# Where the left operands of a seven-product projection are summed and split

## The chip, the cores and the metric

The kernel runs on one core of a Trainium2 chip. The metric is device time in microseconds (us), the median over several runs of the same kernel. The engines are called as in the profile: PE is TensorE (PEld its weight loads), DVE VectorE, ACT ScalarE, POOL GpSimd, SP SyncE, which here only issues DMAs.

## The reference, cut to what matters

One layer of a hybrid decoder trunk is computed in float32: token mixers (gated linear attention, a short convolution, dilated attention), their merge, and then a feed-forward part. The change concerns the feed-forward alone, with 1024 tokens, width 1024 and 2816 hidden channels:

```python
h = rmsnorm(x, pre_ffn_g[l])
gt = causal_dwconv(h @ w_ff_gate[l], ff_conv_w[l]) + ff_conv_b[l]
y = (jax.nn.gelu(gt, approximate=True) * (h @ w_ff_up[l])) @ w_ff_down[l]
x = x + rmsnorm(y, post_ffn_g[l])
```

## The kernel before, in words

**Split.** TensorE gets each float32 operand as two parts, h and l, and a product takes three matmuls: h with h, h with l, l with h. `split` makes the parts: an ACT copy into h (L157), then a DVE subtraction into l (L158).

**Seven of eight.** Large products are taken in 2 x 2 blocks by Winograd's form, with seven block products in place of eight. For that the operands are summed first (A21 + A22, and so on). A block product in the first stage has twelve matmuls of 128 x 128 by 128 x 512.

**First stage: the hidden channels.** The 2816 hidden channels are eleven pairs of 128-channel tiles. Pair 0 is done by plain products (`gemm_by_part`, `gate_or_value`) while `block_sums` makes the sums T1..T4 of the tokens' blocks (tiles FT). Then, for pairs c = 1 to 10, `seven` runs twice: on w_ff_gate (the gate unit) and on w_ff_up (the up unit). One call of `seven`

- loads two 0.5 MB pieces of weights into `raw` tiles (SP issues them; there are three such tiles),
- makes seven left operands: POOL sums blocks of them (L278, L280, L282, L284; into `fb` or in place), and `split` puts them into one of two sets of wh and wl,
- runs seven products into the PSUM banks X, Y and Z. Five reads of a bank stand between products that use the same bank: ACT copies X, Z and X into places of `ring` (L301, L306, L309), DVE adds Y, Z and X to these (L303, L312, L314). So the fifth product of a unit, which writes Z again, cannot start before ACT's read L306 is done; the last cannot before DVE's L314,
- leaves its seventh product for later: it runs right after the first product of the next unit.

As the four blocks (0,0), (0,1), (1,1), (1,0) of a gate unit come out, `conv` makes the convolution and gelu (ACT L1273, DVE L1274 to L1278, ACT L1279). In an up unit DVE multiplies the gate's result by each block (L1314), and the two tiles y of a pair are written to DRAM, to `d_act` (L1317), 0.5 MB each.

**Last stage: back to the model's width.** `down` takes groups of pairs, (0,1), (2,3,4), (5,6,7), (8,9,10), and for each group seven block products in the order 1, 2, 5, 6, 3, 7, 4. For each pair it loads the activations from d_act and the rows of w_ff_down (L1380, all on SP's queue), sums both operands on POOL in place (L1392), splits both (L157, L158) into one of twelve places `ops` (four of them are the tiles wh and wl), and runs the matmuls (L1433): four tiles of tokens, three matmuls for each tile and pair. The result of each tile is added to `acc` by DVE (L1439; in the first group partly copied by ACT, L1438). With the last group `finish` makes the closing norm and residual sum for each of the eight tiles of tokens.

**What sets the order.** The language's scheduler puts the instructions of each engine into one order; each engine then takes its queue in that order and waits on semaphores. `issue_after` in `down` keeps the splits ahead from standing before the sums of results already done (LEAD = 3 products).

## Time and profile before

| what | value |
|---|---|
| time, median of 3 runs (range) | 2009.29 us (2007.48 to 2010.98) |
| span of the profiled execution | 2004.0 us |
| share of the span busy: PE / DVE / ACT / POOL | 95% / 67% / 44% / 38% |
| DMA traffic over the span | 110 GB/s |
| first stage, pairs 1 to 10 | from about 1371 to 1751.56 us of the span |
| last stage, with the finish | from 1751.56 to 2004.0 us |

The profile is of one execution. The device time of that execution is not given apart from its span; the median of the runs is 5.3 us above the span, so what lies around the span is taken as these 5.3 us. Times such as 1536.68 are microseconds from the start of the span. A row of a timeline is one instruction (or x of them run together): its start, its duration, engine, line, operation, out<-in, and in brackets how long the engine was idle before it and what ended that. The rows of PE in a timeline overlap, since matmuls are pipelined: the distance between two starts is what one costs. The shares of busy time are averages over stages with different limits; the stages are read apart below.

### The profile page before, as it was taken

The numbers are of one execution on the slowest core, as the hardware profiler recorded it, in microseconds if no ns is written. First come the engines' busy times: TensorE is split into PE (matmuls) and PEld (weight loads), VectorE is DVE, ScalarE is ACT, GpSimd is POOL, SyncE is SP. The second block draws the span as 40 slices with busy tenths as digits, with TensorE's granted clock in tenths as the row PEclk, the third lists the DMA queues.
The fourth block names the chain that finished last, engine by engine and source line by source line (L and its number), as shares of the span: only waits on it lengthen the run. The fifth ranks groups of instructions, "written<-read, shape, count | busy, mean of one in ns | idle before, by whom it ended". The sixth has DMA issues, their size and how long they took to land. (4 is left out here: it accounts for less than half of the span.)

```text
span 2004.0 us, 25969 instructions
## 1 busy us (share of the span) xinstructions
PE 1902.5 (95%) x9705; PEld 1602.2 (80%) x9705; DVE 1342.6 (67%) x1998; ACT 879.6 (44%) x1620; POOL 764.4 (38%) x456
## 2 busy tenths in 40 slices
PE   6999999999989999999999998998999999989995
PEld 5988788877777899899688776887888888877874
DVE  8756744378888433577545487577666666689998
ACT  5433444455444322435356623344444444454443
POOL 4532323265655331102214562024332322257674
PEclk9999999999999999999999998999999999999998
DMA  4121323323222524213467554221222221443114
GB/s 172 63 84 65 120 95 116 114 97 108 103 84 99 157 77 149 64 38 101 135 202 227 145 190 137 91 88 64 74 95 76 82 95 64 156 160 126 51 76 147
DMA packets 160141, 219.77 MB, mean 110 GB/s; under 512 B 27025, under 2 KB 118031, under 8 KB 160016
## 3 DMA queue, kind: packets, MB, share of 16 engines
q1 hardware_dynamic: 160016, 218.12, 32.8%
q8 instruction: 76, 1.25, 0.3%
q14 instruction: 49, 0.40, 0.1%
HBM read 160.27 MB, written 57.82 MB: 109 GB/s over the span
## 5 line engine op out<-in xcount | busy, mean ns | idle before, releaser
L158 DVE TENSOR_TENSOR wl<-raw,wh 128x512 fp32r<-128x512 f32 (+1 forms) x214 | 211.1, 1019 | 144.9 <-ACT wh L157 144.8
L294 PE MATMUL sX<-T,wh 128*128 128x512 f32 x720 | 227.4, 397 | 17.0 <-DVE ring L314 16.3
L157 ACT ACTIVATE wh<-raw 128x512 fp32r<-128x512 f32 (+1 forms) x226 | 146.3, 671 | 90.2 <-PE sX L294 67.8
L294 PEld LDWEIGHTS sX<-T,wh 128*128 128x128 f32 x720 | 136.1, 191 | 51.6 <-DVE ring L314 22.6
L294 PE MATMUL sX<-FT,wh 128*128 128x512 f32 x480 | 148.1, 390 | 0.9 <-DVE ring L314 0.9
L294 PE MATMUL sX<-T,wl 128*128 128x512 f32 x360 | 141.8, 394 | 0.0
L505 POOL TENSOR_TENSOR fr<-fr 128x512 f32<-128x512 f32 x48 | 72.4, 1507 | 96.3 <-ACT fr L498 92.1
L278 POOL TENSOR_TENSOR fr<-raw 128x512 f32<-128x512 f32 x30 | 40.2, 1339 | 179.9 <-issue 69.1
L278 POOL TENSOR_TENSOR fb<-raw 128x512 f32<-128x512 f32 x20 | 25.8, 1290 | 216.3 <-DMA raw<-in_w_ff_gate_dram 69.2
L158 DVE TENSOR_TENSOR wl<-fr,wh 128x512 fp32r<-128x512 f32 x90 | 64.8, 742 | 63.0 <-ACT wh L157 62.3
L294 PEld LDWEIGHTS sX<-FT,wh 128*128 128x128 f32 x480 | 89.9, 188 | 20.2 <-DVE ring L314 1.6
L157 ACT ACTIVATE wh<-fr 128x512 fp32r<-128x512 f32 (+1 forms) x97 | 62.2, 658 | 81.2 <-PE sX L294 48.1
L294 PE MATMUL sX<-FT,wl 128*128 128x512 f32 x240 | 93.4, 389 | 0.0
L1433 PE MATMUL fX<-ops 128*128 128x512 f32 x336 | 85.4, 399 | 8.2 <-DVE acc L1439 8.2
L1433 PEld LDWEIGHTS fX<-ops 128*128 128x128 f32 x336 | 64.2, 192 | 23.4 <-DVE acc L1439 6.4
L284 POOL TENSOR_TENSOR raw<-raw 128x512 f32<-128x512 f32 x50 | 80.4, 1609 | 0.0
L294 PEld LDWEIGHTS sX<-T,wl 128*128 128x128 f32 x360 | 68.7, 191 | 14.7
L506 DVE TENSOR_TENSOR ring<-ring,fr 128x512 f32<-128x512 f32 x48 | 58.4, 1216 | 28.4 <-POOL fr L505 26.8
L294 PE MATMUL sZ<-T,wh 128*128 128x512 f32 x240 | 73.9, 389 | 0.0
L158 DVE TENSOR_TENSOR ops<-src,ops 128x512 fp32r<-128x512 f32 x77 | 71.7, 967 | 0.0
L1433 PE MATMUL fZ<-ops 128*128 128x512 f32 x264 | 67.5, 398 | 3.8 <-DVE ops L158 2.1
L301 ACT ACTIVATE ring<-sX 128x512 f32<-128x512 f32 x48 | 28.5, 594 | 96.1 <-PE sX L294 75.0
(548 smaller groups left out, 5695.9 us busy)
## 6 DMA issues: line engine op xcount, KB each, us to landing
raw<-in_w_in_dram SPq DMA_DIRECT2D x48, 512.0 KB
raw<-in_w_gate_dram SPq DMA_DIRECT2D x24, 512.0 KB
d_sig<-ring SPq DMA_DIRECT2D x48, 256.0 KB
d_qk<-ring SPq DMA_DIRECT2D x48, 256.0 KB
raw<-in_w_ff_gate_dram SPq DMA_DIRECT2D x22, 512.0 KB
raw<-in_w_ff_up_dram SPq DMA_DIRECT2D x22, 512.0 KB
src<-d_act SPq DMA_DIRECT2D x22, 512.0 KB
src<-in_w_ff_down_dram SPq DMA_DIRECT2D x22, 512.0 KB
```

The source lines that it names most:

```text
L157: S.activation(h, src, AF.Copy)
L158: eng.tensor_tensor(l, src, h.bitcast(F32), op=OP.subtract)
L278: G.tensor_tensor(s1, A21, A22, op=OP.add)
L284: G.tensor_tensor(A21, A11, A21, op=OP.subtract)
L294: PE.matmul(ps, a[x][:, k], b[y][:, k], start=first and k == 0 and n == 0, stop=k == 3 and n == 2, skip_group_check=not first)
L301: S.activation(c11, X, AF.Copy)
L505: G.tensor_tensor(sw, sw, sin[:, hs], op=OP.mult)
L506: V.tensor_tensor(as_(o), as_(o), perm(sw), op=OP.add)
L1433: PE.matmul(ps, o[:, a, ts], o[:, b], start=start and j == 0 and x == 0, stop=j == n - 1 and x == 2, skip_group_check=not start)
```

## The change

The left operands of the last stage's products (of the activations) are no longer made there. They are made in the first stage, as a pair's blocks come out of the up unit: `forms` sums them on POOL in place in the tiles y, `keep` splits each of the seven (ACT copy, DVE subtraction) into one of four staging places and writes h and l together to a new DRAM array `d_fa`, 0.5 MB for each product. The staging places are the rows k = 0 to 3 of F[1] (names F1h, F1l), which nothing reads once `block_sums` is done. `forms` is called as follows: after block (0,0), product 1; after block (1,1), products 4, 5, 7, 6 with the sums a21+a22, a11-a21, s-a11; after block (1,0), product 2, the sum for 3, product 3. For pair 0 all of it runs after `block_sums`. The array d_act and its two writes for each pair are gone.

In the last stage `down` loads h and l of a left operand from d_fa right into the place `ops`, one 0.5 MB load for each pair and product, and sums and splits the right operand alone. The weights' tiles `src` are now six places of one pair each, in place of six of activations and weights together; the tiles of the places `ops` are others in part.

Lines move by one or more: L157/L158 become L158/L159, L301, L306, L309 become L302, L307, L310, L314 becomes L315, L1273 becomes L1274, L1314 becomes L1343.

```diff
-    d_act = dram.tile([FF, T], F32, name="d_act")
+    d_fa = dram.tile([FF // 256, 128, 7, 2, 512], F32, name="d_fa")
...
+    stage = Ring([F[1][i][:, 2 * j:2 * j + 2] for i in range(2) for j in range(2)])
+    PRODUCTS = (1, 2, 5, 6, 3, 7, 4)
+
+    def keep(c, i, ap):
+        o = stage()
+        split(o[:, 0], o[:, 1], ap)
+        nc.sync.dma_start(d_fa[c, :, PRODUCTS.index(i)], o.bitcast(F32))
+
+    def forms(c, y, il):
+        (a11, a21), (a12, a22) = [(t[:, :512], t[:, 512:]) for t in y]
+        if il == (0, 0):
+            keep(c, 1, a11)
+        if il == (1, 1):
+            keep(c, 4, a22)
+            G.tensor_tensor(a22, a21, a22, op=OP.add)
+            keep(c, 5, a22)
+            G.tensor_tensor(a21, a11, a21, op=OP.subtract)
+            keep(c, 7, a21)
+            G.tensor_tensor(a22, a22, a11, op=OP.subtract)
+            keep(c, 6, a22)
+        if il == (1, 0):
+            keep(c, 2, a12)
+            G.tensor_tensor(a12, a12, a22, op=OP.subtract)
+            keep(c, 3, a12)
...
     block_sums(F, fb, FT)
-
-    ring = halves_ring()
+    for il in ((0, 0), (1, 1), (1, 0)):
+        forms(0, ys, il)
+
+    ring = halves_ring(("t2", "t0", "t1"))
...
             V.tensor_tensor(y[i][:, hs], y[i][:, hs], ap, op=OP.mult)
-            if (i, l) in ((0, 1), (1, 0)):
-                r = (2 * c + i) * 128
-                nc.sync.dma_start(d_act[r:r + 128], y[i])
+            forms(c, y, (i, l))
...
-    srcs = []
-    for t in ("G0", "G4", "H0h"):
-        u = slot(t, [128, 2, 2, 2, 512], name="src")
-        srcs.append([u[:, i] for i in range(2)])
...
+    ws = [ap for t in ("G0", "H0h", "H0l") for ap in two(t, (2, 2, 512), F32, "src")]
...
+    places = wpp() + two("G4", (4, 512), F32R, "ops") + wpp()
+    for t in ("G1", "G3", "G2"):
+        places += two(t, (4, 512), F32R, "ops")
...
-            for j in range(n):
-                for x, v in zip(src[j][:2], (v2, w2)):
-                    nc.sync.dma_start(x[:, f].rearrange("p a t -> p (a t)"), v[j][f])
+            for c, (b, _) in zip(cs, src):
+                r = (2 * c + f) * 128
+                nc.sync.dma_start(b[:, f].rearrange("p a t -> p (a t)"), w_fd2[r:r + 128])
...
             if i == 5:
-                sub(s, a21, a22, op=OP.add)
-                sub(b11, b12, b11, eb)
-                return s, b11
+                sub(b11, b12, b11, V if first else G)
             if i == 6:
-                sub(s, s, a11)
                 sub(t, b22, b11)
...
                 o = places()
-                for x, p in enumerate(operands(i, j)):
...
-                        split(o[:, 2 * x], o[:, 2 * x + 1], p)
+                nc.sync.dma_start(o[:, :2].bitcast(F32), d_fa[cs[j], :, PRODUCTS.index(i)])
+                p = right(i, j)
+                with tc.issue_after(taken[order[-1 - LEAD]].ins) if len(order) > LEAD and order[-1 - LEAD] in taken else nullcontext():
+                    split(o[:, 2], o[:, 3], p)
```

**ACT, from an up unit into the next gate unit.** Before, from the gate unit's read of X (L301) to its second read of X (L309); wh<-fb and wh<-raw are copies of splits of the gate unit's weights, L1273 and L1279 the convolution and gelu:

```order
L301 ACTIVATE ring<-sX 128x512
L157 ACTIVATE wh<-fb 128x512
L157 ACTIVATE wh<-raw 128x512 x2
L1273 ACTIVATE fb<-ring,cols 128x512
L306 ACTIVATE ring<-sZ 128x512
L1279 ACTIVATE fb<-fb,cols 128x512
L157 ACTIVATE wh<-raw 128x512
L309 ACTIVATE ring<-sX 128x512
```

After, the same place, and the copies of `keep` (into F1l and F1h, from the tiles y in fb) that stand in it:

```order
L158 ACTIVATE F1l<-fb 128x512
L302 ACTIVATE ring<-sX 128x512
L158 ACTIVATE F1h<-fb 128x512 x2
L158 ACTIVATE F1l<-fb 128x512
L158 ACTIVATE wh<-fb 128x512
L158 ACTIVATE wh<-raw 128x512 x2
L158 ACTIVATE F1l<-fb 128x512
L158 ACTIVATE F1h<-fb 128x512
L1274 ACTIVATE fb<-ring,cols 128x512
L307 ACTIVATE ring<-sZ 128x512
L1280 ACTIVATE fb<-fb,cols 128x512
L158 ACTIVATE wh<-raw 128x512
```

The copies for products 4, 5, 7 and 6 stand around the read of X and ahead of the three weight copies; those for products 2 and 3 stand behind these and ahead of the convolution and the read of Z (L307).

**DVE, the same place.** Before, from the up unit's last sum (L314) to the gate unit's convolution (L1274):

```order
L314 TENSOR_TENSOR ring<-ring,sX 128x512
L1314 TENSOR_TENSOR fb<-fb,ring 128x512
L1314 TENSOR_TENSOR fb<-fb,sX 128x512
L158 TENSOR_TENSOR wl<-fb,wh 128x512
L158 TENSOR_TENSOR wl<-raw,wh 128x512 x2
L303 TENSOR_TENSOR ring<-ring,sY 128x512
L1274 SCALAR_TENSOR_TENSOR fb<-ring,cols,fb 128x511
```

After, from block (1,1) of the up unit (the first L1343 here) on:

```order
L1343 TENSOR_TENSOR fb<-fb,ring 128x512
L159 TENSOR_TENSOR F1l<-fb,F1l 128x512
L159 TENSOR_TENSOR F1h<-fb,F1h 128x512 x2
L1343 TENSOR_TENSOR fb<-fb,sX 128x512
L159 TENSOR_TENSOR F1l<-fb,F1l 128x512
L159 TENSOR_TENSOR wl<-fb,wh 128x512
L159 TENSOR_TENSOR wl<-raw,wh 128x512 x2
L159 TENSOR_TENSOR F1l<-fb,F1l 128x512
L304 TENSOR_TENSOR ring<-ring,sY 128x512
L159 TENSOR_TENSOR F1h<-fb,F1h 128x512
L1275 SCALAR_TENSOR_TENSOR fb<-ring,cols,fb 128x511
```

Between the products of blocks (1,1) and (1,0) stand the splits for products 4, 5 and 7, behind the latter the one for 6; the split for 2 stands ahead of the sum of Y (L304), the split for 3 ahead of the convolution.

**SP's queue, one pair.** Before, from one gate unit's weights to the next:

```order
L168 DMA raw<-in_w_ff_up_dram 128x4x256
L168 DMA raw<-in_w_ff_gate_dram 128x4x256 x2
L168 DMA raw<-in_w_ff_up_dram 128x4x256
L1317 DMA d_act<-fb 128x1024 x2
L168 DMA raw<-in_w_ff_up_dram 128x4x256
```

After:

```order
L169 DMA raw<-in_w_ff_up_dram 128x4x256
L1290 DMA d_fa<-F1l 128x1024 x2
L1290 DMA d_fa<-F1h 128x1024 x2
L1290 DMA d_fa<-F1l 128x1024 x2
L169 DMA raw<-in_w_ff_up_dram 128x4x256
L1290 DMA d_fa<-F1h 128x1024
L169 DMA raw<-in_w_ff_gate_dram 128x4x256 x2
```

The up unit's second load of weights (the last ff_up row) now stands behind six writes to d_fa, and the next gate unit's loads behind the seventh.

## Rows read from the trace of the kernel before

**Rows 1.** Busy time by stretch: time, engines, clock, DMA share, GB/s.
```profile
core 0: us, PE busy (x) PEld busy (x) DVE busy (x) ACT busy (x) POOL busy (x), PEclk, DMA share, GB/s
1360.00:1380.00 20.00, 14.45 (x50) 10.77 (x49) 18.19 (x24) 10.48 (x16) 9.14 (x5) 0.83 0.13 53
1523.08:1561.16 38.08, 38.08 (x169) 31.53 (x168) 23.56 (x37) 16.40 (x28) 11.36 (x8) 1.00 0.25 83
1751.56:1787.52 35.96, 32.94 (x133) 25.53 (x132) 29.69 (x33) 21.39 (x41) 23.13 (x15) 0.95 0.51 176
1787.52:1965.00 177.48, 169.83 (x741) 138.10 (x740) 172.95 (x209) 74.84 (x126) 117.42 (x71) 1.00 0.26 96
1832.00:1852.00 20.00, 18.63 (x83) 15.12 (x82) 20.00 (x29) 8.85 (x15) 7.70 (x6) 1.00 0.79 288
1965.00:1991.00 26.00, 18.93 (x66) 14.00 (x64) 23.82 (x49) 11.84 (x32) 17.90 (x13) 0.87 0.32 117
```

**Rows 2.** Timeline of TensorE, first stage: start, duration, operation.
```profile
1536.68 0.39 PE L294 MATMUL sZ<-F1h,wh 128*128 128x512 f32 x1
...
1539.40 0.62 PE L294 MATMUL sX<-FT,wh 128*128 128x512 f32 x2
...
1544.84 0.62 PE L294 MATMUL sX<-FT,wh 128*128 128x512 f32 x2
```

**Rows 3.** Timeline of DVE, the same stretch.
```profile
1522.48 1.07 DVE L1314 TENSOR_TENSOR fb<-fb,ring 128x512 f32<-128x512 f32 x1
1523.47 0.67 DVE L314 TENSOR_TENSOR ring<-ring,sX 128x512 f32<-128x512 f32 x1
1524.18 0.69 DVE L1314 TENSOR_TENSOR fb<-fb,ring 128x512 f32<-128x512 f32 x1
1528.72 0.69 DVE L1314 TENSOR_TENSOR fb<-fb,sX 128x512 f32<-128x512 f32 x1 [3.85 <-PE sX L294]
1529.33 0.69 DVE L158 TENSOR_TENSOR wl<-fb,wh 128x512 fp32r<-128x512 f32 x1
...
1543.12 0.68 DVE L314 TENSOR_TENSOR ring<-ring,sX 128x512 f32<-128x512 f32 x1
```

**Rows 4.** Timeline of ACT, the same stretch.
```profile
1528.55 0.63 ACT L157 ACTIVATE wh<-fb 128x512 fp32r<-128x512 f32 x1 [1.96 <-PE sX L294]
...
1532.16 0.72 ACT L1273 ACTIVATE fb<-ring,cols 128x512 f32<-128x512 f32 x1 [1.93 <-DVE ring L303]
1534.16 0.60 ACT L306 ACTIVATE ring<-sZ 128x512 f32<-128x512 f32 x1 [1.27 <-PE sZ L294]
...
1536.65 0.63 ACT L157 ACTIVATE wh<-raw 128x512 fp32r<-128x512 f32 x1 [1.28 <-PE sX L294]
1537.19 0.58 ACT L309 ACTIVATE ring<-sX 128x512 f32<-128x512 f32 x1
```

**Rows 5.** Timeline of POOL, the same stretch.
```profile
1521.39 1.61 POOL L282 TENSOR_TENSOR fb<-raw,fb 128x512 f32<-128x512 f32 x1 [1.90 <-DVE wl L158]
1534.81 1.29 POOL L278 TENSOR_TENSOR fb<-raw 128x512 f32<-128x512 f32 x1 [11.82 <-DMA raw<-in_w_ff_up_dram]
1536.18 1.30 POOL L280 TENSOR_TENSOR fb<-fb,raw 128x512 f32<-128x512 f32 x1
```

**Rows 6.** Timeline of SP's queue, the same stretch.
```profile
1530.68 0.38 SPq L168 DMA_DIRECT2D raw<-in_w_ff_up_dram  x1
```

**Rows 7.** Groups by line, 1200 to 2004: busy, mean ns, idle before.
```profile
L158 DVE TENSOR_TENSOR ops<-src,ops 128x512 fp32r<-128x512 f32 x77 | 71.7, 967 | 0.0
```

**Rows 8.** Waits of TensorE, 1787 to 1965: total us, times, longest.
```profile
PE fX L1433 <- DVE acc L1439: 5.4, 4, 1.4
PE fZ L1433 <- DVE acc L1439: 2.2, 3, 1.0
```

**Rows 9.** Timeline of TensorE where the last stage begins.
```profile
1764.02 1.34 PE L1433 MATMUL fZ<-ops 128*128 128x512 f32 x4 [2.07 <-DVE ops L158]
```

More of the change, by code (lines that the diff above doesn't have):

```diff
@@ L1327, in trunk @@
     C11, C12, C21, C22 = [t[:, i] for t in acc for i in range(2)]
-    srcs = []
-    for t in ("G0", "G4", "H0h"):
-        u = slot(t, [128, 2, 2, 2, 512], name="src")
-        srcs.append([u[:, i] for i in range(2)])
-    tmps = [slot(t, [128, 2, 512], name="tmp") for t in ("t0", "t1", "t2")]
-    pairs = Ring([(*u, t[:, 0], t[:, 1]) for u, t in zip(srcs, tmps)])
-    places = [wp.tile([128, 4, 512], F32R, name=n, tag=n) for n in ("wh", "wl")]
-    fb = slot("H0l", [128, 2, 4, 512], F32R, name="ops")
-    places += [fb[:, i] for i in range(2)]
-    places += [wp.tile([128, 4, 512], F32R, name=n, tag=n) for n in ("wh", "wl")]
-    for t in ("G2", "G1", "G3"):
-        fb = slot(t, [128, 2, 4, 512], F32R, name="ops")
-        places += [fb[:, i] for i in range(2)]
+    halves = lambda t: [t[:, i] for i in range(2)]
+    two = lambda t, shape, dt, name: halves(slot(t, [128, 2, *shape], dt, name=name))
+    ws = [ap for t in ("G0", "H0h", "H0l") for ap in two(t, (2, 2, 512), F32, "src")]
+    tmps = [ap for t in ("t0", "t1", "t2") for ap in two(t, (512,), F32, "tmp")]
+    pairs = Ring(list(zip(ws, tmps)))
+    wpp = lambda: [wp.tile([128, 4, 512], F32R, name=n, tag=n) for n in ("wh", "wl")]
+    places = wpp() + two("G4", (4, 512), F32R, "ops") + wpp()
+    for t in ("G1", "G3", "G2"):
+        places += two(t, (4, 512), F32R, "ops")
     places = Ring(places)
@@ L1374, in down, with right, sub @@
         src = [pairs() for c in cs]
[L1375 to L1376 removed]
         for f in range(2):
[L1378 to L1384 removed]
+            for c, (b, _) in zip(cs, src):
+                r = (2 * c + f) * 128
+                nc.sync.dma_start(b[:, f].rearrange("p a t -> p (a t)"), w_fd2[r:r + 128])
+        def right(i, j):
+            b, t = src[j]
             b11, b12, b21, b22 = b[:, 0, 0], b[:, 0, 1], b[:, 1, 0], b[:, 1, 1]
[L1387 removed]
+            def sub(o, x, y, eng=G):
                 if eng is not G:
[L1389 removed]
+                    eng.tensor_tensor(o, x, y, op=OP.subtract)
                     return
                 with tc.issue_after(behind[0].ins) if behind else nullcontext():
[L1392 to L1398 removed]
+                    behind[:] = [eng.tensor_tensor(o, x, y, op=OP.subtract)]
             if i == 5:
[L1400 to L1402 removed]
+                sub(b11, b12, b11, V if first else G)
             if i == 6:
[L1404 removed]
                 sub(t, b22, b11)
[L1406 to L1409 removed]
             if i == 7:
[L1411 removed]
                 sub(b12, b22, b12)
[L1413 to L1415 removed]
+            if i == 4:
+                sub(b21, b21, t)
+            return {1: b11, 2: b21, 5: b11, 6: t, 3: b22, 7: b12, 4: b21}[i]
         def product(i):
@@ L1441, in down @@
         if last:
-            last_x1[:] = [src[j][i][:, f].rearrange("p a t -> p (a t)") for j in range(2) for f in (1, 0) for i in range(2)][:4]
+            last_x1[:] = [b[:, f].rearrange("p a t -> p (a t)") for b, _ in (pairs(), pairs()) for f in range(2)]
         X = [pt("g", "fX") for t in range(4)]
```

24 lines of the change are left out of this document (removed).

## The prediction

> **What bounds the kernel now.** I read the stretches first [rows 1], then one pair of units of the feed-forward's first stage engine by engine [rows 2 to 6], then the last stage [rows 7 to 9].
>
> In the first stage TensorE is busy for the whole of a 38.08 us pair (gate unit, up unit) at a granted clock of 1.00, i.e. at 2.4 GHz, while DVE works 23.56 us, ACT 16.40 and POOL 11.36 [rows 1]. So TensorE is the bound, and there is nothing to win: one product of twelve matmuls takes 2.72 us (1536.68 to 1539.40, [rows 2]), one matmul 0.2267, a pair 14 x 2.72 = 38.08. The other engines look free, but several of them must answer between two products.
>
> In the last stage DVE is the bound. From 1787.52 to 1965 it is busy 172.95 of 177.48 us [rows 1]. The stage has 11 x 7 x 12 = 924 matmuls. Before 1787.52 lie 120 of them (five products of the first two pairs) and the last twelve of the first stage: 132 x 0.2267 = 29.9 us of the 35.96, so the changeover loses 6.0. After 1965 TensorE shows 66 in 26.0 us: 15.0 of work, 11.0 lost. The 738 between are 167.3 of 177.48: 10.2 lost, as stops of at most 1.4 us that end with a sum of DVE's [rows 1, 8]. The whole prize is 27 us, 1.3% of the span.
>
> **The change: the last stage.** Of its 154 splits 77 go (an ACT copy and a DVE subtraction each), and 44 of the POOL sums. The splits into ops from src took 967 ns on DVE [rows 7]. Of the 77 about 60 lay in the middle stretch: 60 x 0.967 = 58 us less for DVE, which falls from 173 to 115 of 167 us. The 10.2 us of stops should then mostly go; I take 8, between 5 (sums still stand behind splits in DVE's order) and 10.2.
>
> The finish (11.0 us) loses its time in the norms and sums of the output, after the splits; the change leaves these instructions as they are. I take 0.
>
> The loads rise from 22 x 0.5 MB of activations to 77 x 0.5 MB of ready operands, with 22 x 0.5 MB of weights: 52 MB in some 215 us, 242 GB/s. The trace moved 288 GB/s at a DMA share of 0.79 [rows 1], so 365 would be full: the loads fit, four products ahead. Only at the changeover do 20 of them come at once, and there the operands of pair 10 are still being made: its last write stands in SP's queue ahead of the load for the third product's second pair. POOL, which no longer waits for activations, starts the weights' sums at once and holds up DVE. Changeover between 4 us better and 5 worse; I take 0.
>
> **The change: the first stage.** Each pair gets 7 ACT copies, 7 DVE subtractions, 4 POOL sums and 7 writes instead of 2. As totals they fit: DVE 23.56 + 7 x 0.69 = 28.4 of 38.08, ACT 16.40 + 7 x 0.63 = 20.8, POOL 11.36 + 4 x 1.30 = 16.6 (durations: [rows 3 to 5]). A staging place comes round after four splits, 5 us or more later; a load took 4.1 us from issue to use [rows 5, 6], so I let no split wait for a write. But they are one chain. POOL sums in place, so it waits until DVE has split what it overwrites; ACT copies only what POOL has summed; and all three take their queues in order. The chain starts with the up unit's block (1,1), and the next gate unit's answers to TensorE stand behind it. I follow it through the traced pair, in the order shown ahead.
>
> DVE ends block (1,1) at 1524.18 + 0.69 = 1524.87 [rows 3]. ACT copy for product 4 to 1525.5, DVE to 1526.3, POOL a21+a22 to 1527.7, ACT copy for 5 to 1528.4. POOL takes a11-a21 from 1527.65 to 1528.95.
>
> Here a price has two ends. DVE ran a product of two SBUF tiles in 1.07 us (from 1522.48) while POOL's op lasted from 1521.39 to 1523.00; alone the same took 0.69, and reading PSUM at 1523.47 it wasn't held [rows 3, 5]. So DVE waits for POOL's op to end, then takes 0.6. The Trainium skill, "SBUF — State Buffer", section "SBUF: two separate sides", says so: DVE and GpSimd share a port pair under an exclusive lock, and who comes second is blocked for the whole instruction. The trace agrees (DVE ended 0.55 us after POOL); by that rule the pair below loses the larger sum, without it the smaller. I take the held durations, since the row is of this stage.
>
> So DVE's split for 5 waits to 1528.95 and ends 1529.55. POOL's sum for 6 runs 1529.65 to 1530.95, DVE's split for 7 to 1531.55. Block (1,0), at 1528.72 before, now ends at 1532.2, and the split for 6 at 1532.75. ACT copies 6 to 1531.65, then the three weight copies that stood at 1528.55 [rows 4] to 1533.3, then 2 to 1533.9. DVE's three weight splits and the split for 2 end at 1535.2, POOL's last sum at 1536.6, ACT's copy for 3 at 1537.3. Only now come ACT's convolution start (1532.16 before) to 1537.9 and its read of bank Z (1534.16 before) to 1538.5. TensorE wants Z at 1536.68 [rows 2]: **first stop, 1.8 us.**
>
> The rest is 3.5 us late on ACT: the weight copy of 1536.65 starts at 1540.15, and the read of X after it ends at 1541.25 where TensorE, itself 1.8 late, wants it at 1541.2. DVE's sum out of X, which stands behind what hangs on that copy, ended at 1543.80 [rows 3]; 3.5 later it is 1547.3. TensorE wants X at 1544.84 + 1.9 = 1546.75: second stop, 0.6. That is 2.5 us a pair. If the up unit's second weight load, at 1530.68 before and 4.1 us from POOL's use [rows 5, 6], now behind product 2's write, goes out at 1535.7, POOL sums at 1539.8 amid DVE's splits, and X is ready at 1548.8: 4.0 a pair. With every op at its price alone the first chain takes 12.4 us from 1524.87, so Z at 1537.3 (0.65 late) and X about 0.7 later: 1.4 a pair. I take 3.0, between 2.5 and 4.0. A stop of 2.07 us that ended at 1764.02 [rows 9] was followed by a stretch at half clock (1.2 GHz; clock 0.95 in the changeover's row, [rows 1]), stops up to 1.4 left it at 1.00 [rows 1, 8]; at 1.8 it may happen, but then TensorE wants X some 1.7 us later too, and the pair still ends at 3.5 to 4.0.
>
> Pairs 1 to 9 are followed by a gate unit: **9 x 3.0 = 27 us.** Pair 0's seven splits fall where DVE is busy 18.19 of 20 us and the clock 0.83 [rows 1]: between 3 (as any pair) and 10 (7 splits at the held 1.4); I take 7. In the up units the one added split, for product 1, ends on ACT about a microsecond before Z is wanted: 0.
>
> **Sum.** 27 + 7 - 8 + 0 + 0 = +26 us. The profiled execution spans 2004.0 us, the median is 5.3 above it; what lies around the span stays: 2009.3 + 26 = **2035 us.**
>
> **Rivals.** (a) *The chain at its prices alone*: if DVE and POOL don't hold each other: 9 x 1.4 + 5 - 8 = +10, 2019. Against it: the 1.07 us row. (b) *The chain in full*, weights late and the clock dropped at the stops: 9 x 4.0 + 10 - 5 = +41, 2050. For it: 4.1 us from issue to use; against it: the up unit has idle time on every engine, in which a delay is paid back before the next pair. (c) *Faster*: the chain ends inside the idle time of the gate unit, since 11.8 us lie between 1524.87 and 1536.68; nothing stops in the first stage, and the last gains 8 to 10 and the changeover 3: 1996 to 2001. It decides at Z: ACT's read of it would have to end by 1536.7, against the 1537.3 that even the unheld chain gives. (d) *The last stage waits for its loads*: 242 GB/s wanted against 288 seen; were they late at every group's start by a write and read of about 5 us, 4 x 5 = 20 lost and the 8 not won: 34 + 20 = +54, 2063. Against it: places for four products ahead.
>
> **How the numbers follow.** Forecast 0.55, (a) 0.20, (b) 0.13, (c) 0.07, (d) 0.05. The range takes in (a) and (b) with the bounds: below, 9 x 1.4 + 3 - 10 - 4 = +2; above, 9 x 4.0 + 10 - 5 + 5 = +46: 2010 to 2056. About 0.2% (4 us) is what a measurement here can tell from no change: faster 0.08, same 0.05 (the lower edge of (a)), slower 0.87.
>
> **What would show it.** Right: TensorE stops near 1.8 us before the gate unit's fifth product that end with ACT's read of Z, and shorter ones before the last that end with DVE's sum out of X; pairs of about 41 us; DVE's 512-column splits at 1.1 to 1.7 us beside POOL's sums; the last stage with fewer stops on DVE in its middle and the same 11 us lost at its finish. Wrong: pairs of 38.1 us at clock 1.00 (then (c)), or TensorE waiting in the last stage for loads of ready operands (then (d)).

## The result, and the profile after

The changed kernel takes 2045.84 us (median of 4 runs, 2042.78 to 2047.08), the kernel before 2009.69 in the same comparison. The ratio is 1.0185, with an interval of 1.0172 to 1.0197: slower, by 36 us. The profiled execution spans 2045.1 us against 2004.0. It took 2046.83 us, so 1.7 us lie around its span, and not the 5.3 that were taken for the kernel before; by this estimate the profiled execution of that kernel took 2005.7 us, some 3.6 less than its median. Of these 41.1 us, 3.0 lie ahead of the feed-forward, where both kernels have the same instructions (its first matmul starts at 1322.19 against 1319.22; in the runs below it lies between 1317.8 and 1323.4). They are scatter. The other 38.1 are of the feed-forward. From the starts of the same matmuls in both traces (a unit is marked by its second product, the last stage by the 133rd and the 861st of its 924 matmuls):

| stretch | before | after | difference | predicted |
|---|---|---|---|---|
| first matmul of the feed-forward to gate unit 1 | 50.58 | 50.60 | 0.0 | 0 |
| gate unit 1 to gate unit 2 (end of pair 0, pair 1) | 44.48 | 52.54 | +8.1 | +7 |
| gate unit 2 to the last up unit (nine gate units) | 323.68 | 364.15 | +40.5 | +27 |
| last up unit to the 133rd matmul (changeover) | 53.68 | 54.01 | +0.3 | 0 |
| 133rd to 861st matmul (middle of the last stage) | 173.58 | 166.02 | -7.6 | -8 |
| 861st matmul to the end (finish) | 38.75 | 35.55 | -3.2 | 0 |

The prediction let the middle begin twelve matmuls earlier, at 1787.52. Cut there, the changeover goes from 49.56 to 51.29 us (+1.7) and the middle from 177.70 to 168.74 (-9.0): a stop before the 133rd matmul, which is gone, lies between the two cuts.

First the stretches, as in [rows 1]: one pair of the first stage, then changeover, middle and finish.

```profile
core 0: us, PE busy (x) PEld busy (x) DVE busy (x) ACT busy (x) POOL busy (x), PEclk, DMA share, GB/s
1552.16:1593.91 41.75, 38.86 (x169) 31.30 (x168) 30.61 (x43) 20.29 (x35) 17.44 (x13) 1.00 0.38 138
1806.50:1843.49 36.99, 34.77 (x142) 27.71 (x143) 20.04 (x28) 17.29 (x31) 11.77 (x9) 0.95 0.82 321
1843.49:2009.51 166.02, 165.52 (x729) 136.51 (x728) 102.05 (x143) 42.41 (x71) 53.69 (x38) 1.00 0.70 254
2009.51:2045.00 35.49, 16.88 (x65) 12.35 (x63) 31.38 (x70) 12.38 (x36) 19.93 (x15) 0.81 0.40 148
```

A pair lasted 38.08 us with TensorE busy throughout [rows 1]; now it lasts 41.75 with TensorE busy 38.86 and no engine near full: DVE works 30.61 us of it, ACT 20.29, POOL 17.44. In the middle of the last stage DVE has fallen from 173 of 177 us [rows 1] to 102 of 166, and TensorE is busy for 165.52 of 166.02. The waits of TensorE from 1420 to 1800 (engine, line, what it waited for: us in total, times, longest):

```profile
PE sX L295 <- DVE ring L315: 15.2, 9, 1.9
PE sZ L295 <- ACT ring L307: 15.0, 9, 1.7
```

Nine stops end with ACT's read of bank Z and nine with DVE's sum out of bank X, one of each in every gate unit from 2 to 10. These are the two places that [rows 2 to 4] showed as served in time. In the middle of the last stage nothing of more than 0.25 us is left in place of [rows 8].

Now one pair, the rows that answer to [rows 2 to 6], from the timeline of each engine (start, duration, instruction, idle time before it and what ended that).

```profile
1561.98 0.50 PE L295 MATMUL sZ<-F1h,wh 128*128 128x512 f32 x1 [1.50 <-ACT ring L307]
...
1572.01 0.73 PE L295 MATMUL sX<-FT,wh 128*128 128x512 f32 x2 [1.38 <-DVE ring L315]
```

```profile
1547.85 0.69 DVE L1343 TENSOR_TENSOR fb<-fb,ring 128x512 f32<-128x512 f32 x1
...
1551.99 3.13 DVE L159 TENSOR_TENSOR F1l<-fb,F1l 128x512 fp32r<-128x512 f32 x2 [2.05 <-ACT F1l L158]
1555.04 0.67 DVE L1343 TENSOR_TENSOR fb<-fb,sX 128x512 f32<-128x512 f32 x1
...
1558.05 0.68 DVE L159 TENSOR_TENSOR F1h<-fb,F1h 128x512 fp32r<-128x512 f32 x1
...
1571.28 0.68 DVE L315 TENSOR_TENSOR ring<-ring,sX 128x512 f32<-128x512 f32 x1
```

```profile
1560.20 0.63 ACT L158 ACTIVATE F1l<-fb 128x512 fp32r<-128x512 f32 x1 [2.88 <-POOL fb L1307]
1560.74 0.71 ACT L1274 ACTIVATE fb<-ring,cols 128x512 f32<-128x512 f32 x1
1561.35 0.58 ACT L307 ACTIVATE ring<-sZ 128x512 f32<-128x512 f32 x1
```

```profile
1551.37 1.28 POOL L1301 TENSOR_TENSOR fb<-fb 128x512 f32<-128x512 f32 x1
1553.29 1.29 POOL L1303 TENSOR_TENSOR fb<-fb 128x512 f32<-128x512 f32 x1 [0.63 <-DVE F1l L159]
1558.87 1.30 POOL L1307 TENSOR_TENSOR fb<-fb 128x512 f32<-128x512 f32 x1 [4.30 <-DVE F1h L159]
1563.25 1.29 POOL L279 TENSOR_TENSOR fb<-raw 128x512 f32<-128x512 f32 x1 [3.08 <-DMA raw<-in_w_ff_up_dram]
```

```profile
1559.17 0.39 SPq L169 DMA_DIRECT2D raw<-in_w_ff_up_dram  x1
```

The chain can be read across the fences. DVE ends block (1,1) at 1548.54. POOL's sums for products 7 and 6 run to 1552.65 and 1554.58; DVE's two splits (3.13 us for two subtractions that take 0.69 each alone) end at 1555.12, about 0.5 us after the second sum. The split for product 2 ends at 1558.73, POOL takes its last sum from 1558.87 to 1560.17, ACT copies that at 1560.20, starts the convolution and reads Z by 1561.93, and TensorE starts at 1561.98 after 1.50 us of idle time. On SP the up unit's second load of weights goes out at 1559.17; POOL's sum of these weights, idle for 3.08 us until they land, starts at 1563.25, and the sum out of X ends at 1571.96. TensorE follows at 1572.01.

### The profile page after: what moved, and what is told of

The parts are those of the page before. It is cut to its first block, busy times and chain, and to the rows that moved or that the text cites. A ratio compares the mean times of both kernels' runs of the same rounds, so it can differ in the third digit from the quotient of the medians.

```text
span 2045.1 us, 26258 instructions
## 1 busy us (share of the span) xinstructions
PE 1916.1 (94%) x9705; PEld 1607.6 (79%) x9705; DVE 1339.7 (66%) x1998; ACT 879.1 (43%) x1620; POOL 752.8 (37%) x456
## 4 chain that ended last, share of the span: by engine, by line
PE 56%; DVE 21%; issue 7%; POOL 6%; ACT 5%; DMA 4%; SPq 0%; DVEq 0%; POOLq 0%; ACTq 0%
PE sX L295 13%; DVE wl L159 6%; PE sZ L295 6%; PE fX L1442 5%; PE sY L295 4%; PE fZ L1442 4%; PE vX L563 3%; POOL fr L506 2%; PE vZ L563 2%; PE p L198 1%; PE p L200 1%; PE p L202 1%; ACT wh L158 1%; PE mx L1225 1%; PE mx L1226 1%
## 5 line engine op out<-in xcount | busy, mean ns | idle before, releaser
L159 DVE TENSOR_TENSOR wl<-raw,wh 128x512 fp32r<-128x512 f32 (+1 forms) x214 | 214.8, 1035 | 113.9 <-ACT wh L158 100.6
L158 ACT ACTIVATE wh<-raw 128x512 fp32r<-128x512 f32 (+1 forms) x226 | 146.2, 670 | 72.0 <-PE sX L295 52.4
L295 PE MATMUL sX<-FT,wh 128*128 128x512 f32 x480 | 153.8, 402 | 17.5 <-DVE ring L315 16.2
L295 PEld LDWEIGHTS sX<-FT,wh 128*128 128x128 f32 x480 | 90.7, 192 | 43.5 <-DVE ring L315 20.5
L159 DVE TENSOR_TENSOR wl<-fr,wh 128x512 fp32r<-128x512 f32 x90 | 64.8, 742 | 62.9 <-ACT wh L158 62.2
L158 ACT ACTIVATE wh<-fr 128x512 fp32r<-128x512 f32 (+1 forms) x97 | 62.2, 658 | 80.8 <-PE sX L295 48.0
L283 POOL TENSOR_TENSOR fr<-raw,fr 128x512 f32<-128x512 f32 x30 | 49.7, 1658 | 48.9 <-DVE wl L159 48.9
L1413 POOL TENSOR_TENSOR src<-src 128x512 f32<-128x512 f32 x20 | 29.6, 1505 | 95.1 <-DVE ops L159 73.1
```

What stands on the lines that cost most here:

```text
L158: S.activation(h, src, AF.Copy)
L159: eng.tensor_tensor(l, src, h.bitcast(F32), op=OP.subtract)
L283: G.tensor_tensor(s1, A12, s2, op=OP.subtract)
L295: PE.matmul(ps, a[x][:, k], b[y][:, k], start=first and k == 0 and n == 0, stop=k == 3 and n == 2, skip_group_check=not first)
L1413: behind[:] = [eng.tensor_tensor(o, x, y, op=OP.subtract)]
```

## The experiments

The theory: the added work runs as one chain through ACT, DVE and POOL, all in order, and what the next gate unit owes TensorE stands behind it. By this, ACT's queue (copies ahead of the read of Z) makes the first stop, and SP's queue (the up unit's second load behind six writes) sets the size of the second. The rivals: the added instructions are too much as such; or the added DMA traffic is in the way; or only POOL's part of the chain costs. All runs are compared with the kernel before on their own chip. The scheduler sets the order anew for each of them, so a run can move more than its edit says. "Pair" is the distance from one gate unit to the next for c = 2 and on, 38.08 us before; after, 42.17 on average of the seven pairs at a granted clock of 1.00, and 44.08 for the eighth.

**1. Z is read first.** The tail of the chain (product 2's split, the last sum, product 3's split) goes behind the read of Z on ACT; the load stays behind product 2's write.

```diff
-        S.activation(c22, Z, AF.Copy)
+        zi = S.activation(c22, Z, AF.Copy)
+        with tc.issue_after(zi.ins):
+            while later:
+                later.pop(0)()
...
-            keep(c, 2, a12)
-            G.tensor_tensor(a12, a12, a22, op=OP.subtract)
-            keep(c, 3, a12)
+            def tail():
+                held.append(keep(c, 2, a12))
+                G.tensor_tensor(a12, a12, a22, op=OP.subtract)
+                keep(c, 3, a12)
+            later.append(tail)
```

> Only the order on ACT is changed: the copies for products 2 and 3 and the POOL sum between them stand behind the gate unit's read of Z; the up unit's second load still stands behind product 2's write on SP's queue. Chain theory (two separate causes: ACT's order sets the stop at Z, the late load sets the stop at X): the Z stops of 1.85 us go to 0.5 or less, but the sum out of X still comes 19.8 us after the start of the unit's second product against the 16.3 at which TensorE, no longer late, wants it; so the X stops grow from 1.85 to about 3.5 and the pair stays near 41.6 to 42.2 us: 2040 to 2047 us. Rival (the two stops are independent, each worth its own length): 10 x 1.85 less, 2026 to 2029 us.

Measured: 2042.27 us, 1.0177 [1.0162, 1.0192]; pairs of 41.6 to 42.4 us. TensorE's waits, 1420 to 1745:

```profile
PE sX L298 <- DVE ring L321: 12.0, 7, 2.0
PE sX L298 <- ACT ring L316: 10.0, 8, 1.3
PE sZ L298 <- ACT ring L310: 2.1, 4, 0.9
```

The stops at Z are nearly gone (2.1 us in four), so the order on ACT made them. Little is won by it: ACT's second read of X, which TensorE wants 2.7 us after Z, now stops it (L316), since the copy for product 3 stands ahead of that instead, and the stop at DVE's sum stays. The time is the expected one; that the loss would gather in one stop of about 3.5 us at DVE's sum isn't what happened.

**2. The load first.** The writes of products 7, 6, 2 and 3 stand behind the up unit's second load on SP; everything else as in the changed kernel.

```diff
+        if src is w_fu2:
+            with tc.issue_after(loads[-1].ins):
+                while writes:
+                    writes.pop(0)()
...
+        if c > 0 and i in (7, 6, 2, 3):
+            writes.append(write)
+        else:
+            write()
```

> Only SP's order is changed: the writes of products 7, 6, 2 and 3 stand behind the up unit's second load of weights. Chain theory: the load goes out 3 us or more sooner, POOL's weight sums no longer fall among DVE's splits; the Z stops stay at 1.85, the X stops fall from 1.85 to 0.5 to 0.8, the pair to about 40.6 us: 2030 to 2036 us. Rival (the X stop comes from ACT's lateness alone): no change, 2044 to 2047 us.

Measured: 2038.61 us, 1.0153 [1.0136, 1.0170]; pairs of 41.3.

```profile
PE sZ L301 <- ACT ring L313: 11.6, 8, 1.7
PE sX L301 <- ACT ring L316: 5.6, 7, 0.8
PE sX L301 <- DVE ring L321: 1.3, 1, 1.3
```

The stop at DVE's sum is gone but for one, so the late load made it. The Z stop stays as expected. A new, smaller one comes up at ACT's second read of X (L316), so a pair gains 0.8 us and not the 1.5 that was expected. In the pair around 1565 the weights have landed early, POOL sums them from 1561.54, and one step of DVE's convolution beside that (L1283) takes 1.66 us in place of 0.75; the read of X stands behind it on ACT.

**3. Both.** The two edits together.

> Both orders are changed. Chain theory: Z stops 0.5 or less and X stops 1.0 or less, pairs of 38.1 to 39.5 us, 24 to 36 us less than the changed kernel: 2010 to 2022 us. Rival (the added work and DVE waiting for POOL set the pair, not the order): pairs above 40.5 us, 2032 us or more.

Measured: 2071.67 us, 1.0322 [1.0307, 1.0338], the slowest of all. TensorE has one stop a pair:

```profile
PE sX L301 <- ACT ring L319: 34.5, 7, 5.1
```

The timelines of POOL and ACT in one pair:

```profile
1567.12 1.28 POOL L285 TENSOR_TENSOR fb<-raw 128x512 f32<-128x512 f32 x1 [7.29 <-DVE F1h L159]
...
1570.92 1.26 POOL L1323 TENSOR_TENSOR fb<-fb 128x512 f32<-128x512 f32 x1
...
1572.22 0.63 ACT L158 ACTIVATE F1l<-fb 128x512 fp32r<-128x512 f32 x1 [5.09 <-POOL fb L1323]
1572.75 0.58 ACT L319 ACTIVATE ring<-sX 128x512 f32<-128x512 f32 x1
```

Both stops of the changed kernel are gone and a longer one has taken their place. With the load early, the scheduler put POOL's three weight sums (from 1567.12) ahead of the sum for product 3 (1570.92). ACT, in order, stands 5.09 us at the copy of that sum with the read of X right behind it. The expectation failed in sign: it counted the two causes as terms that add up. Each edit alone moves the chain; the two together changed who stands ahead of whom on POOL.

**4. The last stage alone.** No left operand is made in the first stage, except that one split of pair 0 is written to all seven places, which the last stage then loads for every pair.

```diff
-    for il in ((0, 0), (1, 1), (1, 0)):
-        forms(0, ys, il)
+    o = stage()
+    split(o[:, 0], o[:, 1], ys[0][:, :512])
+    for i in range(7):
+        nc.sync.dma_start(d_fa[0, :, i], o.bitcast(F32))
...
-            forms(c, y, (i, l))
+            pass
...
-                nc.sync.dma_start(o[:, :2].bitcast(F32), d_fa[cs[j], :, PRODUCTS.index(i)])
+                nc.sync.dma_start(o[:, :2].bitcast(F32), d_fa[0, :, PRODUCTS.index(i)])
```

> The first stage makes no operands (forms is left out, but for one split of pair 0 written seven times) and the last stage loads these stand-ins in place of the real left operands, so the output is not the reference's. It measures the gain of the last stage by itself. From the trace of the changed kernel: changeover 0, middle -7.6, end of TensorE's work -3.9, finish +0.7, pair 0 about +1: 1998 to 2002 us. If the gain of the last stage needed the longer first stage, it would be nearer 2009.

Measured: 2000.61 us, 0.9968 [0.9957, 0.9979]. A pair and the middle of the last stage, in the columns of the windows above:

```profile
1538.44:1576.52 38.08, 38.08 (x170) 31.53 (x168) 23.38 (x36) 16.41 (x28) 10.91 (x8) 1.00 0.17 56
1796.82:1962.88 166.06, 165.56 (x729) 136.51 (x728) 101.50 (x142) 40.86 (x68) 54.02 (x38) 1.00 0.66 232
```

The pairs are back at 38.08, and the middle is the 166.06 of the changed kernel (166.02): the loss sits in the first stage, the gain in the last, and they don't touch each other. Here the changeover is 4.7 us shorter as well (from the last stage's first matmul to the 133rd 35.34 against 40.08 us). In the changed kernel TensorE stops there for 4.7 us in all, at DVE's sums and for two loads of ready operands:

```profile
1804.75 0.73 PE L1442 MATMUL fX<-wh 128*128 128x512 f32 x2 [1.47 <-DMA wh<-d_fa]
1827.05 3.00 PE L1442 MATMUL fZ<-wl 128*128 128x512 f32 x12 [0.93 <-DMA wl<-d_fa]
```

Run 4 has none of these stops. That they come from pair 10's operands, which are still being made there, is likely; no run left out those alone. Pair 0 lost 8.0 us in this run too, by its own doing: seven writes stand back to back on SP, ahead of the up unit's load, and a stop of 7.89 us of TensorE ends with the sum out of X that hangs on these weights.

```profile
1378.36 6.38 SPq L1329 DMA_DIRECT2D d_fa<-F1h  x7
1384.86 1.13 SPq L169 DMA_DIRECT2D raw<-in_w_ff_up_dram  x1
```

Without that the last stage alone is worth about 16 us: 7.5 in the middle, 4.7 at the changeover, 3.6 at the finish. That is nearly 60% of the prize that the prediction had put at 27 us.

**5. Small writes.** From pair 1 on a write carries 16 of 512 columns; all else as in the changed kernel, with all loads from pair 0's part.

```diff
-        nc.sync.dma_start(d_fa[c, :, PRODUCTS.index(i)], o.bitcast(F32))
+        n = 512 if c == 0 else 16
+        nc.sync.dma_start(d_fa[c, :, PRODUCTS.index(i), :, :n], o.bitcast(F32)[:, :, :n])
```

> For pairs 1 to 10 the writes to DRAM carry 16 of the 512 columns (1/32 of the bytes); number, place in SP's queue and waits stay, and the last stage loads pair 0's operands in place of the other pairs', so the output is not the reference's. Order theory: the up unit's second load is late because it stands behind writes that wait for their splits, not because of their bytes: Z stops near 1.85, X stops 1.5 to 1.9, pairs 41.5 to 42.3 us, 2040 to 2047 us. Rival (traffic: 35 MB more written delays the weights): X stops under 0.7, pairs under 41 us, 2025 to 2034 us.

Measured: 2047.67 us, 1.0201 [1.0186, 1.0216]: as slow as with the whole traffic. The window of a pair at full clock, and TensorE's waits:

```profile
1467.04:1508.87 41.83, 38.69 (x169) 31.39 (x168) 31.65 (x44) 20.20 (x35) 17.26 (x13) 1.00 0.19 53
```

```profile
PE sX L295 <- ACT ring L310: 14.4, 8, 1.8
PE sZ L295 <- ACT ring L307: 11.3, 8, 1.5
```

The DMA share is 0.19 in place of 0.38, the stop at Z is there, and a pair is as long (41.8 us). So traffic is not the cause of the first stop, nor of the length of a pair. The second stop is not the one of the changed kernel, though: it ends with ACT's second read of X (L310) and not with DVE's sum. The order on SP came out otherwise than expected, with the up unit's second load at 1557.87, ahead of product 2's write. POOL then sums these weights from 1561.49 on, beside DVE's convolution, whose two steps take 1.76 and 1.67 us in place of 0.75; ACT's read waits behind them, as in run 2. What the small writes alone would do to the stop at DVE's sum stays open. Five of the eight pairs have a stretch at half clock and last 43.5 to 43.6 us.

**6. No sums.** POOL's four sums are left out; the seven copies, subtractions and writes stay.

```diff
-            G.tensor_tensor(a22, a21, a22, op=OP.add)
...
-            G.tensor_tensor(a21, a11, a21, op=OP.subtract)
...
-            G.tensor_tensor(a22, a22, a11, op=OP.subtract)
...
-            G.tensor_tensor(a12, a12, a22, op=OP.subtract)
```

> The four POOL sums of the first stage are left out (the seven operands are split and written unsummed, so the output is not the reference's); copies, subtractions and writes stay. Chain theory: without the sums nothing in the chain waits for POOL, ACT reads Z in time, and the weights' load goes out earlier: Z stops under 0.5, X stops under 1, pairs 38.1 to 39.5 us, 2010 to 2022 us. Rival (seven more copies and subtractions alone fill ACT and DVE at the wrong time): pairs above 40.5 us, 2032 us or more.

Measured: 2005.67 us, 0.9992 [0.9981, 1.0004], pairs of 38.08 to 38.33 and one of 38.91:

```profile
1537.04:1575.14 38.10, 38.10 (x170) 31.49 (x168) 29.54 (x44) 20.44 (x35) 11.68 (x8) 1.00 0.42 152
```

This is the run that tells most. ACT and DVE do all the work that the change gave them (20.44 and 29.54 us of a pair, almost what they do in the changed kernel) and the writes go out, yet TensorE hardly stops (0.4 us in all from 1420 to 1745). It went better than any theory expected. What costs 4 us a pair are the four sums, in the place where they stand.

**7. The sums on DVE.** `G.tensor_tensor` becomes `V.tensor_tensor` in the same four lines.

> The four sums of the first stage are made by DVE in place of POOL: two engines instead of three in the chain, no DVE work held by POOL's, 4 x 0.69 us more on DVE. Chain theory, worked with the unheld prices (0.6 to 0.7 us each): ACT's read of Z ends 0.3 us before TensorE wants it, X at most 0.6 late: pairs 38.1 to 39.0 us, 2010 to 2020 us. Rival (DVE's order becomes the bound): pairs 40.5 us or more, 2032 us or more.

Measured: 2010.09 us, 1.0009 [0.9997, 1.0021], pairs of 38.8 to 39.2, no stop at Z, and at X

```profile
PE sX L295 <- DVE ring L315: 4.6, 8, 0.8
```

near what was expected (at most 0.6). The same arithmetic on the engine that already has the chain costs about 0.9 us a pair in place of 4.1: a sum takes 0.69 and not 1.3, no split is held beside it, and two changes of engine fall away for each sum.

**8. The chain in steps.** POOL keeps the sums, but they and the splits are spread over the gate unit, each behind one of its reads (the split for 7 behind the read of Y, those for 6 and 2 behind Z, that for 3 behind X); the load is early, the writes late.

```diff
...
+            def y_():
+                keep(c, 7, a21)
+                G.tensor_tensor(a21, a12, a22, op=OP.subtract)
+            def z_():
+                keep(c, 6, a22)
+                keep(c, 2, a12)
+            todo.extend((y_, z_, lambda: keep(c, 3, a21)))
...
```

> The operands are made in steps placed where nothing of the gate unit stands behind them: splits for 4 and 5 at once; 7 behind the sum of Y; 6 and 2 behind the read of Z; 3 behind the first read of X; the sum for 3 goes to another place, ahead of POOL's weight sums; the writes of 5, 7, 6, 2 and 3 stand behind the up unit's second load. Order theory: the same work without the stops, pairs 38.1 to 39 us; pair 0 still 7 to 9 and the changeover as in the changed kernel: 2005 to 2014 us. Rival (some other in-order wait takes the place, as when both orders were changed before): pairs above 40 us, 2025 us or more.

Measured: 2025.73 us, 1.0092 [1.0075, 1.0109], pairs of 40.3 to 40.5 and two, with a stretch at half clock, of 41.8 and 41.9, against an expected 2005 to 2014:

```profile
PE sX L302 <- DVE ring L323: 14.3, 8, 2.1
```

The Z stop is gone, the stop at DVE's sum is as large as ever. In its new place of the queue the chain meets POOL's last sum and the weight sums: between 1549.15 and 1556.9 a step of the convolution and three subtractions on DVE take 1.8 us each, beside POOL's four operations of 1.3 to 1.74 us from 1549.13 on. DVE is held as before, mostly by other operations of POOL's.

**9. Short sums.** POOL's four sums over 64 of 512 columns (0.32 to 0.75 us each, in place of 1.3); no other line is changed.

```diff
-            G.tensor_tensor(a22, a21, a22, op=OP.add)
+            G.tensor_tensor(a22[:, :64], a21[:, :64], a22[:, :64], op=OP.add)
...
```

> The four POOL sums of the first stage take 64 of the 512 columns (the rest stays unsummed, so the output is not the reference's): the chain keeps every step from engine to engine, its order and its writes, but POOL's part is short and can hold DVE only briefly. Theory of the length (1.3 us of POOL each, and DVE held for the same time, in a chain ahead of the reads): Z stops under 0.6, X stops under 1, pairs 38.1 to 39.3 us, 2004 to 2018 us, near the run without sums. Rival (the steps from engine to engine, with their waits, cost most): pairs above 40 us, 2026 us or more.

Measured: 2016.01 us, 1.0039 [1.0026, 1.0053]; pairs of 39.2 to 40.0.

```profile
PE sX L295 <- ACT ring L310: 8.6, 7, 1.7
PE sX L295 <- DVE ring L315: 1.2, 1, 1.2
```

The time lies in the expected range, the pairs and the stops at X above it. Short sums take off about 2.5 of the 4.1 us a pair, and the stop at Z is gone altogether, although every step from engine to engine is still there. So that stop hangs on the length of the sums, with what DVE waits beside them, and not on the steps as such. (In part the order came out otherwise too: the up unit's second load stands ahead of product 2's write, and ACT's convolution ahead of the copy for product 3.) The stop that is left is another one, at ACT's second read of X. The rows of the pair in which one such stop, of 1.66 us, ends at 1551.40:

```profile
1546.08 1.76 DVE L159 TENSOR_TENSOR F1l<-fb,F1l 128x512 fp32r<-128x512 f32 x1 [0.88 <-ACT F1l L158]
1547.76 1.77 DVE L1276 SCALAR_TENSOR_TENSOR fb<-ring,cols,fb 128x510 f32<-128x510 f32 x1
...
1546.00 1.29 POOL L279 TENSOR_TENSOR fb<-raw 128x512 f32<-128x512 f32 x1 [0.62 <-DMA raw<-in_w_ff_up_dram]
1547.37 1.62 POOL L281 TENSOR_TENSOR fb<-fb,raw 128x512 f32<-128x512 f32 x1
...
1549.63 0.72 ACT L1280 ACTIVATE fb<-fb,cols 128x512 f32<-128x512 f32 x1 [3.10 <-DVE fb L1276]
```

The weights have landed early here too, and DVE's split for product 3 and the convolution are held beside POOL's weight sums (1.76 and 1.77 us in place of 0.69 and 0.75). Runs 2, 5 and 9 thus share one new stop. No run separates the length of POOL's sums from what DVE waits beside them, so how the loss at Z divides between the two stays open.

**10 and 11. DVE's sums, better ordered.** In 10 the sums are on DVE, the writes stand behind the load, and pair 0's last splits stand behind ACT's second read of X. In 11 the sums are on DVE and the chain in steps as in 8. In both the first places of the last stage are other tiles.

> Sums on DVE as in the run before, and besides: the writes of 7, 6, 2 and 3 behind the up unit's second load; pair 0's products 6, 2 and 3 behind the first gate unit's read of X; the first places of the last stage are tiles that come free one product after the last up unit's start. Theory: X stops 0.6 to 0.9 go (9 x 0.75 = 6.8 us less), pair 0 costs 2 to 5 instead of 7, the stop of 2.5 at the changeover goes: 1994 to 2001 us, faster than both kernels. Rival (another in-order wait takes the place, as twice before): 2005 us or more.

> As the run before, but the splits for 7, 6, 2 and 3 and their sums (on DVE) stand behind the gate unit's weight splits and its sum of Y, so that the weights' raw tiles come free and the up unit's second load goes out as in the kernel before. Order theory: the X stops of 0.5 us vanish, pairs of 38.1 to 38.4 us, 4 to 6 us less than the run before: 2000 to 2003 us. Rival (DVE has now too much between the sum of Y and the sum out of X): X stops of 0.5 us or more, 2006 us or more.

Measured: 2006.29 us, 0.9988 [0.9975, 1.0002] for 10 (pairs of 38.7 to 39.0; the stretch with the end of pair 0 costs 2.4 and not 8.1), and 2015.40 us, 1.0030 [1.0019, 1.0040] for 11 (pairs of 39.77). The waits of TensorE in 10, then in 11:

```profile
PE sX L301 <- DVE ring L324: 3.1, 8, 0.5
```

```profile
PE sX L302 <- DVE ring L323: 11.1, 8, 1.4
```

Run 10 was expected at 1994 to 2001 and can't be told from the kernel before: DVE's sum out of X still comes 0.5 us late in each pair, so some 6 us of the first stage stand against the gain of the last. In run 11 the rival came out: moved into the gate unit, DVE's splits run beside POOL's weight sums again (1.66 to 1.78 us each).

**12. Only what needs no sum.** The kernel before, where from pair 1 to 9 the left operands of products 1, 2 and 4 (a block by itself, no sum) are split and written in the first stage and loaded ready in the last; products 3, 5, 6 and 7 are made in the last stage as before.

```diff
+    def keep(c, i, ap):
+        if c in READY_C:
+            o = stage()
+            split(o[:, 0], o[:, 1], ap)
+            nc.sync.dma_start(d_fa[c, :, READY.index(i)], o.bitcast(F32))
...
+            if (i, l) != (0, 1):
+                keep(c, {(0, 0): 1, (1, 1): 4, (1, 0): 2}[i, l], y[i][:, hs])
...
+                    if x == 0 and i in READY and cs[j] in READY_C:
+                        nc.sync.dma_start(o[:, :2].bitcast(F32), d_fa[cs[j], :, READY.index(i)])
+                        continue
```

> The kernel before with one part of the change: for pairs 1 to 9 only the operands that need no sum (products 1, 2 and 4) are split and stored in the first stage, three copies, three subtractions and three writes a pair, no POOL sum; d_act, the sums and all other splits stay in the last stage, whose loads of these three come ready. Theory (the POOL sums in the chain cost the first stage, and the middle of the last stage needs only part of DVE's relief): pairs 38.1 to 38.3 us, pair 0 and changeover as before; 27 of the 60 splits in the middle gone, 26 us less of DVE's 173, so its 10.2 us of stops mostly go: middle -5 to -8, end -1 to -4, first stage +0 to +2: 1997 to 2004 us, faster than the kernel before. Rival (any extra split in the first stage stops TensorE, or the last stage gains only when all splits go): 2006 to 2014 us.

Measured: 2002.57 us, 0.9979 [0.9966, 0.9991], a little faster than both kernels. A pair and the middle of the last stage:

```profile
1531.66:1569.74 38.08, 38.08 (x170) 31.54 (x168) 26.15 (x39) 18.12 (x31) 11.73 (x8) 1.00 0.35 124
1794.35:1964.36 170.01, 166.20 (x730) 136.35 (x728) 151.54 (x181) 62.44 (x105) 116.48 (x71) 1.00 0.44 167
```

The pairs stay at 38.08, and the middle falls from 173.58 to 170.01 us: 3.6, where 5 to 8 were expected. The finish gives 1.4; the other stretches differ by up to 2 us either way.

## Why the prediction was right, and where it wasn't

**The mechanism held, and step by step.** The prediction followed the chain through a pair. With its times moved by 23.67 us, so that block (1,1) ends together with the measured one, they can be put beside the trace:

| step | predicted | measured |
|---|---|---|
| DVE's split for product 2 ends | 1558.87 | 1558.73 |
| up unit's second load goes out | 1559.37 | 1559.17 |
| POOL's last sum ends | 1560.27 | 1560.17 |
| ACT's read of Z ends | 1562.17 | 1561.93 |
| POOL's first sum of the late weights | 1563.47 | 1563.25 |
| X ready, with the late load | 1572.47 | 1571.96 |
| X ready, without it | 1570.97 | |

No step is off by more than 0.3 us up to the last, which is 0.5 early (this pair is the shortest of the seven undisturbed ones, 41.75 us). The held price was the right choice: the two splits of 3.13 us end half a microsecond after POOL's operation, as [rows 3, 5] had it once. The Trainium skill ("SBUF — State Buffer", section "SBUF: two separate sides") calls this an exclusive lock between a DVE operation with two inputs in SBUF and a POOL operation that reads SBUF; the trace agrees, at 1.2 to 1.8 us for a subtraction that takes 0.69 alone. Rival (a), the chain without it, fell. Rival (c) fell at Z, where it was to be decided: the read ended 1.5 us late. Rival (d) fell too: in the middle TensorE waits for nothing over 0.25 us. At the changeover it does wait for ready operands, 2.4 us in all.

One reading of rows was wrong, with a right result: that DVE isn't held when it reads PSUM doesn't follow from the operation at 1523.47, since POOL's had ended at 1523.00. In the kernel before it follows from one that ran while POOL's was running (1521.39 to 1523.00) and took no longer than alone:

```profile
1521.77 0.67 DVE L312 TENSOR_TENSOR ring<-ring,sZ 128x512 f32<-128x512 f32 x1
```

**The step that was mis-sized: "I take 3.0, between 2.5 and 4.0".** Measured are 4.09 us a pair (42.17 against 38.08). The upper bound hung on an "if": the up unit's second load behind product 2's write. That was no open question. SP's queue in the part on the change showed the load behind six writes, and the predicted time of the write gave the time of the load to within 0.2 us. So 4.0 was the term, and 2.5 was a case that the order had already excluded. Run 2 says the same from the other side: with the load ahead of the writes, the stop at DVE's sum out of X is gone. But 2.5 was too low for its own case as well: a pair of run 2 still loses 3.3 us, with a stop at ACT's second read of X that the prediction didn't have. Between 3.0 and 4.0 lie 9 us over nine gate units, of the 13.5 that this stretch lost beyond its term; the 0.09 above 4.0 is 0.8 more.

**The clock.** The remaining 3.7 us (40.5 less nine times 4.09) lie in the two pairs in which TensorE ran at half clock (1.2 GHz) for 3.4 us after a stop; half of that is lost each time, 3.4 us in both. The prediction named this and let it cost nothing beyond a pair's 3.5 to 4.0: the clock was to fall at the stop at Z, and the later stop at X would take it up. Both times it fell at the stop at X, behind which nothing takes it up. The timeline at one of the two stops, then the windows of this one and of a stretch with stops that left the clock alone:

```profile
1741.09 0.76 PE L295 MATMUL sX<-FT,wh 128*128 128x512 f32 x2 [1.87 <-DVE ring L315]
```

```profile
1738.84:1745.08 6.24, 4.37 (x13) 3.13 (x12) 3.77 (x7) 2.62 (x4) 0.48 (x1) 0.73 0.00 0
1443.60:1450.00 6.40, 4.56 (x20) 3.49 (x19) 4.41 (x9) 3.88 (x7) 0.45 (x1) 1.00 0.00 0
```

**The last stage.** The middle came out as said: 7.6 us won, or 9.0 by the prediction's own cut, against 8, with nearly no stops left. The busy time of DVE fell further than said, to 102 us and not 115, which changed nothing, since TensorE had become the bound. The finish, put at 0 because "the change leaves these instructions as they are", gave 3.2 us, and the sign "the same 11 us lost at its finish" failed with it. TensorE's stops there were 1.43, 2.70 and 3.20 us before and 0.72, 1.49 and 3.25 after, 1.9 less; some 2 us more come from less time at half clock behind them (granted clock 0.87 before, 0.93 after, over TensorE's part), and what follows its last matmul is 0.7 longer. Why the stops are shorter isn't shown; the last splits that stood ahead of these instructions are fewer. The changeover's 0 came near (+0.3, or +1.7 by the prediction's cut) by luck, as the sum of a gain and a loss: run 4 shows 4.7 us of gain there when the first stage makes no operands.

**Pair 0.** +8.1 against 7, between 3 and 10. All of it lies in the first gate unit (33.50 us against 25.44): a new stop of 5.04 us at ACT's read of Z, one of 1.27 at its second read of X, and more time at half clock (granted clock 0.85 against 0.87). Run 10, whose edits include moving that pair's last splits, brought it to 2.4, run 6 without sums to 4.6.

**The sum.** Predicted +26: 27 + 7 - 8. Measured in the same terms +38: 40.5 + 8.1 + 0.3 - 7.6 - 3.2. The forecast's direction and mechanism were right; its main term was too small by a third, because a bound that the queue had decided was averaged. The nearest case at the result is rival (b), the chain in full, at 2050.

## What to carry to other kernels

Work moved under a stage that TensorE bounds is free only if it doesn't stand ahead of an answer that TensorE waits for: follow it through the in-order queue of each engine, SP's among them, up to the first such answer, and where the order shows an "if" as decided, take that end as the term. Seven more copies, subtractions and writes a pair cost next to nothing here; four sums on POOL, each of which waits for DVE, is waited for by ACT and holds DVE meanwhile, cost 4 us. So move first what needs no third engine (run 12), look for what POOL will run beside DVE when a load comes earlier (runs 2, 5, 9), and don't expect that removing one late step wins its time: in runs 1, 2, 3, 8 and 11 the next step in the same queues came up in its place.

## What the runs showed of the hardware

- Stops of nearly the same length had different effects on TensorE's clock: of the 18 stops of 1.4 to 1.9 us in gate units 2 to 10 16 left it at 1.00 and two were followed by 3.4 us at half clock; in run 3 each of the nine stops of about 5 us came with 3.4 to 6.8 us at half clock. What tells the two of 18 apart, and why run 5 shows it in five of eight pairs, stays open.
- Seven 0.5 MB writes that are ready together occupy SP's queue for 6.38 us (run 4), and a load of weights behind them goes out that much later. Writes of 16 columns in place of 512 (run 5) left the stop at Z as it was.
- Not only subtractions are held beside POOL. Between 1410 and 1750 the longer steps of the convolution on DVE take 0.75 us in both kernels, but 1.1 to 1.9 us 22 times in run 1, 16 times in run 5, 12 in run 8 and 7 to 9 in runs 2, 9 and 10, each time with an operation of POOL's beside them.
- The idle time shown before a matmul is less than the stop costs. At the stop of 1.50 us in the pair above the start comes 1.89 us after the one before it, in place of 0.23, and the next one 0.34 after that; so a pair lost 4.1 us where the idle times listed add up to some 3.4.
